# A first stage fed by 2 MB halves of the modulation weights and single K tiles, and precedence for emptying the mixers' PSUM banks

## The chip, the cores and the metric

One core of a Trainium2 chip runs the whole program. The metric is the device time of one execution in microseconds (us). TensorE (PE) multiplies, VectorE (DVE) and ScalarE (ACT) compute elementwise, GpSimd (POOL) does a little, and SyncE (SP) issues the DMAs. Every engine runs its own queue in order and waits at semaphores for the others.

## The reference

Two layers over 1024 tokens of width 2048, all in float32. In each layer:

```
mod = silu(c) @ w_mod + b_mod;  shift, scale, gate = split(mod, 3)
h   = rms_norm(x, g_pre) * (1 + scale) + shift
a_q, a_k, a_v, s_u, s_v, c_q, c_k, c_v, c_g, z = split(h @ w_in)
y_a = sliding_window_attention(rope(a_q), rope(a_k), a_v, sinks)     # 16 heads of 64, window 128
y_b = gelu(s_u) * (causal w_s @ layer_norm(gelu(s_v)) + b_s)          # chunks of 128
y_c = rms_norm(gated_linear_attention(c_q, c_k, c_v, log_sigmoid(c_g @ w_up + b) / 16), gla_norm_g)
out = (concat(y_a, y_b, y_c) * silu(z)) @ w_out
x   = x + gate * rms_norm(out, g_post)
```

## The kernel before

The work is cut into four phases: two layers, and in each two halves of 512 tokens. A phase has an input part (`in_phase`) and an output part (`out_phase`). Both are made of column groups: for each of 16 K tiles of 128 input features, four (or fewer) PSUM banks of the pool `pj` (6 banks) get three matmuls each. Three, because float32 is kept by splitting: each weight tile and each activation tile is cut into a high part (a cast on ACT, L368 for weights) and a low part (a subtraction on DVE, L369), and high x high, high x low and low x high are summed. `mm_f` (L382 to L384) writes features by tokens, `mm_t` (L390 to L392) tokens by features. A split activation tile is called a slot, in pool `act`; the raw weights sit in pool `wraw` (2 buffers), the split ones in `whl` (3 buffers), fetched two K tiles at a time.

The mixers (attention, spatial gating, gated linear attention) are generators on lanes. `tick()` is called after each three matmuls of a group, and a lane goes on when the number of ticks that its generator last yielded has passed. `LAG` holds such distances for attention: after the scores of two blocks ("s"), before the transposes ("e"), and after each of the two blocks of transposes ("t"). The mixers' matmuls write to the two banks of pool `mx`, and DVE or ACT must empty a bank before the next mixer matmul can have it: the scores are taken by L498/L500 (ACT) and L501 (DVE), the transposes of the probabilities M (L533) by the multiplication with the mask into PT (L535, DVE), the products PT x v (L546) by L549 (ACT), the scores of the linear attention by L617 (DVE), its output after the transposes L558 by ACT.

The order in each engine's queue is set by a scheduler: it takes instructions as written, by precedence and by its own picture of what is ready. Code in `urgent()` gets a precedence higher by `PRIO`, 300 instructions. The splits of weights already stand in it.

The modulation of later chunks (`mod_chunk`, L225 on DVE) also runs on a lane, fed by loads `wm` of 256 KB.

The first stage is written apart. Layer 0 needs `acol` and `bcol` (scale and shift by feature) before any slot can be made, and these need 8 chunks of 4 MB of `w_mod`. PE multiplies them with silu(c) spread over 32 columns (`scb`), two K tiles a load of 512 KB (L1107), the four 32-row strips of one bank taking K tiles in turn; `mod_columns` transposes the sums (L197) and makes two columns of acol and bcol. Meanwhile x, loaded with tokens on the partitions, is squared and summed on ACT (L1054), scaled on POOL (L283), transposed on PE (L1084), scaled and shifted on DVE (L1086) and split. `work()` puts the projection of the first five output blocks (512 columns of group "kcq" and 128 of `w_ck`) between the products, one block of three matmuls at a time. The sixth block (128 more columns of `w_ck`) follows in `in_phase` by `proj_f(P)`. Then comes the group `w_vcg` of 272 columns.

After the group "zc" (the z of the linear attention), `gla_c` loads gla_norm_g into a tile of pool `t2`, multiplies it into z (L820) and that into the output (L822), and transposes the result (`tok_to_y`, L558). In the same stretch the second attention of the phase is at work.

## Time and profile before

| | us |
|---|---|
| median of 3 runs | 3127.75 (3121.66 to 3129.04) |
| profiled execution, its own time | 3122.08 |
| its span | 3120.4 |
| PE busy | 3042.7 (98%) |
| DVE busy | 1837.3 (59%) |
| ACT busy | 1206.2 (39%) |
| mean granted PE clock | 0.991 |
| DMA moved | 469 MB, mean 150 GB/s |

How to read what follows. A row of the timeline gives the start, the duration, the engine, the line of the kernel, the operation, the tile written and read, the shape, the count of merged instructions (x4), and in brackets how long the engine sat idle before it and what ended that. Matmuls are pipelined: the durations of neighbours overlap, and the distance of two starts is what one costs. A row of the stages gives from:to, the length, then busy time and count for PE, weight loads (PEld), DVE, ACT and POOL, the granted PE clock (1.00 is full), the share of time that the DMA engines were busy, and GB/s. A row of waits reads: who <- for whom: us in total, times, longest.

### The profile page before, as it was taken

What the parts mean: (1) busy time and instruction counts of PE and PEld (TensorE: products, weight loads), DVE (VectorE), ACT (ScalarE), POOL (GpSimd) and SP (SyncE); (2) the same over time, 40 slices, a digit from 0 to 9 for tenths busy, and PEclk for the clock granted to TensorE, in tenths of its full rate; (3) what the DMA queues carried; (4) which work ended last, traced back from release to release, by engine and by line L of the source; (5) the groups of instructions that cost most, each with busy time, mean ns of one, the idle gap of its engine ahead of it and who ended that gap; (6) DMA issues with size and microseconds to landing.
All of it is one profiled execution on the core that took longest, in us unless ns stands there. A gap on an engine that the chain in (4) does not pass through costs nothing.

```text
span 3120.4 us, 44382 instructions
## 1 busy us (share of the span) xinstructions
PE 3042.7 (98%) x17346; PEld 2448.0 (78%) x17346; DVE 1837.3 (59%) x2957; ACT 1206.2 (39%) x2399; POOL 43.4 (1%) x84
## 2 busy tenths in 40 slices
PE   6999999999999999999999999999999999999998
PEld 2477778888878787888888878788888888788886
DVE  3358768565676877745355676644346486663425
ACT  3145437332344443423234554432223544442323
POOL 2000000000000000000000000000000000000000
PEclk8999999999999999999999999999999999999999
DMA  9754446566676435544446323334446332343535
GB/s 330 240 163 140 145 135 206 169 203 203 200 237 197 131 120 178 173 135 149 122 123 190 95 75 94 115 109 142 119 124 203 97 89 85 108 120 113 164 107 165
DMA packets 224195, 468.99 MB, mean 150 GB/s; under 512 B 21584, under 2 KB 77296, under 8 KB 223984
## 3 DMA queue, kind: packets, MB, share of 16 engines
q1 hardware_dynamic: 223984, 466.15, 48.7%
q8 instruction: 136, 2.23, 0.3%
q14 instruction: 75, 0.61, 0.1%
HBM read 429.37 MB, written 36.70 MB: 149 GB/s over the span
## 4 chain that ended last, share of the span: by engine, by line
PE 82%; DVE 8%; DMA 5%; ACT 2%; issue 2%; SPq 0%; DVEq 0%; ACTq 0%
PE pj L382 13%; PE pj L383 12%; PE pj L384 12%; PE pj L390 12%; PE pj L392 12%; PE pj L391 12%; DMA wm<-in_w_mod_dram 2%; PE mx L546 2%; PE mx L492 2%; PE pj L1107 1%; DVE whl L369 1%; DMA t<-in_gla_norm_g_dram 1%; DVE ma L225 1%; DMA t<-in_x_dram 1%; PE mx L533 1%
## 5 line engine op out<-in xcount | busy, mean ns | idle before, releaser
L369 DVE TENSOR_TENSOR whl<-wraw,whl 128x1024 fp32r<-128x1024 f32 (+3 forms) x512 | 590.6, 1154 | 730.6 <-ACT whl L368 728.0
L368 ACT CAST whl<-wraw 128x1024 fp32r<-128x1024 f32 (+3 forms) x512 | 509.1, 995 | 1097.0 <-PE pj L392 515.5
L390 PE MATMUL pj<-whl,act 128*128 128x512 f32 (+1 forms) x2048 | 785.5, 384 | 1.0 <-ACT whl L368 1.0
L392 PE MATMUL pj<-whl,act 128*128 128x512 f32 (+1 forms) x2048 | 777.8, 380 | 0.0
L391 PE MATMUL pj<-whl,act 128*128 128x512 f32 (+1 forms) x2048 | 775.3, 379 | 1.2 <-DVE whl L369 1.2
L382 PE MATMUL pj<-act,whl 128*128 128x512 f32 x1904 | 751.6, 397 | 3.6 <-ACT whl L368 2.0
L383 PE MATMUL pj<-act,whl 128*128 128x512 f32 x1904 | 745.3, 391 | 0.3 <-DVE act L279 0.3
L384 PE MATMUL pj<-act,whl 128*128 128x512 f32 x1904 | 744.5, 391 | 0.5 <-DVE whl L369 0.5
L392 PEld LDWEIGHTS pj<-whl,act 128*128 128x128 f32 x2048 | 385.4, 188 | 73.2 <-issue 1.2
L390 PEld LDWEIGHTS pj<-whl,act 128*128 128x128 f32 x2048 | 385.3, 188 | 72.7 <-issue 5.6
L391 PEld LDWEIGHTS pj<-whl,act 128*128 128x128 f32 x2048 | 385.5, 188 | 68.5 <-DVE whl L369 1.9
L382 PEld LDWEIGHTS pj<-act,whl 128*128 128x128 f32 x1904 | 357.5, 188 | 101.3 <-issue 20.3
L384 PEld LDWEIGHTS pj<-act,whl 128*128 128x128 f32 x1904 | 358.1, 188 | 83.7 <-issue 7.1
L383 PEld LDWEIGHTS pj<-act,whl 128*128 128x128 f32 x1904 | 358.2, 188 | 77.7 <-issue 6.2
L225 DVE SCALAR_TENSOR_TENSOR ma<-wm,sc,ma 128x512 f32<-128x512 f32 x240 | 179.7, 749 | 102.5 <-DMA wm<-in_w_mod_dram 100.1
L517 ACT ACTIVATE M<-M,at_nm 128x128 f32<-128x128 f32 x256 | 99.4, 390 | 46.7 <-DVE at_nm L509 42.2
L535 DVE TENSOR_TENSOR PT<-mx,amask 128x1024 f32<-128x1024 f32 x64 | 78.1, 1220 | 22.6 <-PE mx L533 22.6
L1107 PE MATMUL pj<-wm,scb 128*32 128x512 f32 x256 | 67.0, 665 | 24.2 <-DMA wm<-in_w_mod_dram 24.2
L501 DVE COPY_PREDICATED M<-pmask,mx 128x256 f32<-128x256 uint8 x128 | 51.6, 442 | 57.3 <-ACT M L500 48.5
L546 PE MATMUL mx<-PT,v 128*64 128x128 f32 x960 | 68.4, 288 | 13.9 <-DVE PT L535 13.9
L546 PEld LDWEIGHTS mx<-PT,v 128*64 128x64 f32 x960 | 57.5, 143 | 28.3 <-DVE PT L535 16.3
L500 ACT COPY M<-mx 128x256 f32<-128x256 f32 x96 | 32.1, 375 | 101.0 <-PE mx L492 100.7
(230 smaller groups left out, 2421.9 us busy)
## 6 DMA issues: line engine op xcount, KB each, us to landing
wraw<-in_w_in_dram SPq DMA_DIRECT2D x312, 512.0 KB, 3.6
wraw<-in_w_out_dram SPq DMA_DIRECT2D x136, 512.0 KB, 3.6
wm<-in_w_mod_dram SPq DMA_DIRECT2D x256, 256.0 KB, 3.3
wm<-in_w_mod_dram SPq DMA_DIRECT2D x64, 512.0 KB, 6.2
y<-at SPq DMA_DIRECT2D x64, 256.0 KB, 2.7
q<-y SPq DMA_DIRECT2D x64, 256.0 KB, 3.3
q<-x SPq DMA_DIRECT2D x36, 256.0 KB, 2.8
wraw<-in_w_vcg_dram SPq DMA_DIRECT2D x32, 272.0 KB, 2.8
```

The lines of the kernel that those rows point to most:

```text
L225: V.scalar_tensor_tensor(acc, ws[k], sc[:, k:k + 1], acc, ALU.mult, ALU.add)
L368: S.copy(hl[:, 0], raw)
L369: V.tensor_tensor(hl[:, 1], raw, hl[:, 0].bitcast(F32), ALU.subtract)
L382: PE.matmul(ps, lhsT=whi, rhs=slot[:, 0], start=(k == 0), stop=False)
L383: PE.matmul(ps, lhsT=whi, rhs=slot[:, 1], start=False, stop=False)
L384: PE.matmul(ps, lhsT=wlo, rhs=slot[:, 0], start=False, stop=(k == NK - 1))
L390: PE.matmul(ps, lhsT=slot[:, 0, c], rhs=whi, start=(k == 0), stop=False)
L391: PE.matmul(ps, lhsT=slot[:, 0, c], rhs=wlo, start=False, stop=False)
L392: PE.matmul(ps, lhsT=slot[:, 1, c], rhs=whi, start=False, stop=(k == NK - 1))
L517: S.activation(Mf[:, k], Mf[:, k], AF.Exp, bias=nm[:, k:k + 1], scale=0.125, accum_out=den[:, k:k + 1])
L546: PE.matmul(yp[64 * p:64 * p + 64, n * P:(n + 1) * P], lhsT=vv[:, g * 64:g * 64 + 64], rhs=pts[p][:, w, n], start=(w == 0), stop=(w == 1 o ...
L1107: PE.matmul(mps[r:r + 32, :], lhsT=scb[:, k], rhs=w[:, kk], start=(k < 4), stop=(k >= 12))
```

## The change

The first stage is rewritten, and instructions that empty the mixers' banks get precedence.

First stage:
- x comes with features on the partitions (`x_f` now holds both halves), eight loads of 512 KB ahead of everything else; it stays in eight tiles of pool `act`. No transposes of x.
- The sum of squares: ACT squares, DVE adds pairs, PE sums over the partitions by eight products with ones into one bank. The root is taken over 512 columns (`r0`).
- The modulation's weights come as 16 halves of 2 MB (3 buffers), eight products in a row for each, into a bank of `mx`.
- The weights of the projection come one K tile at a time (512 columns of "kcq" and all 256 of `w_ck`), queued behind the halves. `project(k)` does all six blocks of a K tile, so `in_phase` has nothing left to do for `w_ck` in the first phase.
- `fill` scales by acol and r0 (DVE), casts the high part with the shift added (ACT) and makes the low part (DVE). All of it is in `urgent()`.
- The tables of sines and cosines for the first half are made after the sixth chunk.

Mixers: `urgent()` around the emptying of the scores, of the transposes into PT, of PT x v, of the transposes to y, of the linear attention's scores and outputs, and of the spatial gating; "t" in LAG goes from (3, 5) to (3, 8); `gla_c` waits 5 more ticks before its transposes.

```diff
-LAG = {"s": (3, 4), "e": 14, "t": (3, 5)}
+LAG = {"s": (3, 4), "e": 14, "t": (3, 8)}
...
-    def rsqrt(out, src, n):
+    def rsqrt(out, src, n, pool=sm):
...
-            dst = out if it == 2 else sm.tile([P, n], F32, tag="rq_y", name="rq_y")
+            dst = out if it == 2 else yv
...
-                for p in range(2):
-                    sp = sps[p]
...
+                with urgent():
+                    for p in range(2):
+                        sp = sps[p]
...
-                V.tensor_tensor(pt, tp.rearrange("p (n q) -> p n q", n=NT).unsqueeze(1).broadcast_to([P, 2, NT, P]),
-                                amask.unsqueeze(2).broadcast_to([P, 2, NT, P]), ALU.mult)
+                with urgent():
+                    V.tensor_tensor(pt, tp.rearrange("p (n q) -> p n q", n=NT).unsqueeze(1).broadcast_to([P, 2, NT, P]),
+                                    amask.unsqueeze(2).broadcast_to([P, 2, NT, P]), ALU.mult)
...
-        ps = ps[4:] + proj_f(P, slots) if pre else proj_f(256, slots)
-        ck = evac(2, hold, ps)
+        ck = evac(2, hold, ps[4:] if pre else proj_f(256, slots))
...
                 V.tensor_tensor(of, of, zt[n], ALU.mult)
                 yield 2
+            yield 5
             yield from tok_to_y(h, [o.rearrange("p h d -> p (h d)") for o in outs], 12)
...
+        xq = [act_p.tile([P, 2, H], F32, tag="act", name="xq") for _ in range(8)]
+        for c in range(8):
+            load(xq[c], a["x_f"][0, 2 * c:2 * c + 2].rearrange("j p t -> p j t"))
...
+        def first_load(k):
+            if k < NK:
+                r = wraw_p.tile([P, 1, 768], F32, tag="wraw", name="wraw")
+                load(r[:, 0, 0:512], a["w_in"][0, 0, :, k])
+                load(r[:, 0, 512:], a["w_ck"][0, :, k])
+                raw_q.append(r)
...
+        def mod_load(c, part):
             if c < 8:
...
+                w = st.tile([P, 8, 512], F32, name="wm0", bufs=3)
+                load(w, a["w_mod"][0, c, :, 8 * part:8 * part + 8])
                 ws.append(w)
...
+        for c in range(8):
+            sq = st.tile([P, 2, H], F32, name="sq", bufs=2)
+            S.activation(sq, xq[c], AF.Square)
+            s2 = st.tile([P, H], F32, name="s2", bufs=2)
+            V.tensor_tensor(s2, sq[:, 0], sq[:, 1], ALU.add)
+            PE.matmul(sums, lhsT=ones, rhs=s2, start=(c == 0), stop=(c == 7))
+        r0 = st.tile([P, H], F32, name="r0")
+        V.tensor_scalar(r0, sums, 1.0 / D, EPS, ALU.mult, ALU.add)
+        rsqrt(r0, r0, H, st)
...
+        def mod_products(mps, part):
+
+            w = ws.popleft()
+            for kk in range(8):
+                k = 8 * part + kk
+                r = 32 * (k % 4)
+                PE.matmul(mps[r:r + 32, :], lhsT=scb[:, k], rhs=w[:, kk], start=(k < 4), stop=(k >= 12))
+
+        def fill(c, mps):
+            acc = st.tile([P, 512], F32, name="mod_acc", bufs=2)
+            S.copy(acc, mps)
             mod_columns(0, c, acc, 4)
...
+                V.scalar_tensor_tensor(xt, xq[c][:, j], acol[0][:, k:k + 1], r0, ALU.mult, ALU.mult)
+                s = act_p.tile([P, 2, 512], F32R, tag="act", name="act")
+                S.activation(s[:, 0], xt, AF.Identity, bias=b)
+                V.scalar_tensor_tensor(s[:, 1], xt, b, s[:, 0].bitcast(F32), ALU.add, ALU.subtract)
...
         for c in range(8):
+            if c:
+                mod_load(c, 1)
+                first_load(2 * c - 1)
+            mps = mxt()
+            mod_products(mps, 0)
+            if c:
+                project(2 * c - 2)
+                mod_load(c + 1, 0)
+                first_load(2 * c)
+            mod_products(mps, 1)
             with urgent():
+                fill(c, mps)
+            if c:
+                project(2 * c - 1)
+            if c == 5:
+                for _ in rope_tables(0):
                     pass
+        first_load(NK - 1)
+        project(NK - 2)
+        project(NK - 1)
```

The same `urgent()` stands around the emptying L549, L560, L617 and the others named above.

What this does to the queues is shown at three places. Lines are numbered by each kernel's own text; for the rows shown the changed kernel's numbers are lower by one (L369 is L368, L546 is L547), or higher by two to four behind the new `urgent()` lines (L558 is L560, L820 and L822 are L824 and L826).

SP's queue at the start of the program, before. `wm` are the modulation's weights, `x` the tokens, `raw_a` and `raw_b` the weights of the first projection.

```order
L58 DMA wm_190<-in_w_mod_dram 128x1024
L58 DMA x_0_169<-in_x_dram 128x4x512
L58 DMA x_1_170<-in_x_dram 128x4x512
L58 DMA x_2_171<-in_x_dram 128x4x512
L58 DMA x_3_172<-in_x_dram 128x4x512
L58 DMA t_196<-in_positions_dram 128x512
L58 DMA raw_a<-in_w_in_dram 128x1024
L58 DMA raw_b<-in_w_ck_dram 128x2x128
L58 DMA wm_293<-in_w_mod_dram 128x1024
```

The same queue now, `xq` being x with features on the partitions.

```order
L57 DMA xq<-in_x_f_dram 128x2x512 x8
L57 DMA wm_187<-in_w_mod_dram 128x4096
L57 DMA wm_189<-in_w_mod_dram 128x4096
L57 DMA wm_191<-in_w_mod_dram 128x4096
L57 DMA wraw<-in_w_in_dram 128x512
L57 DMA wraw<-in_w_ck_dram 128x256
L57 DMA wm_300<-in_w_mod_dram 128x4096
L57 DMA wraw<-in_w_in_dram 128x512
```

Eight loads of the modulation stood ahead of x before; now all of x goes first, and each half of the modulation is followed by one K tile of weights.

DVE's queue behind the z group of the third phase, before: the two PT multiplications of an attention step, the z and norm products L820 and L822, and a split of weights.

```order
L535 TENSOR_TENSOR PT<-mx,amask 128x1024
L820 SCALAR_TENSOR_TENSOR hold<-hold,t_16620 128x512
L535 TENSOR_TENSOR PT<-mx,amask 128x1024
L822 TENSOR_TENSOR hold<-hold 128x512
L820 SCALAR_TENSOR_TENSOR hold<-hold,t_16620 128x512
L369 TENSOR_TENSOR whl<-wraw,whl 128x1024
```

And now.

```order
L536 TENSOR_TENSOR PT<-mx,amask 128x1024
L824 SCALAR_TENSOR_TENSOR hold<-hold,t_16396 128x512
L536 TENSOR_TENSOR PT<-mx,amask 128x1024
L826 TENSOR_TENSOR hold<-hold 128x512
L824 SCALAR_TENSOR_TENSOR hold<-hold,t_16396 128x512
L368 TENSOR_TENSOR whl<-wraw,whl 128x1024
```

The order is the same here, as in the second and fourth phase; in the first phase both PT multiplications now stand ahead of the first L824.

PE's queue at the same place, before: products PT x v (L546), the projection of the next group (L390 to L392) and the transposes of the linear attention's output (L558).

```order
L391 MATMUL pj<-whl,act 128x512
L392 MATMUL pj<-whl,act 128x512
L546 MATMUL mx<-PT,v 64x128
L390 MATMUL pj<-whl,act 128x512
L391 MATMUL pj<-whl,act 128x512
L546 MATMUL mx<-PT,v 64x128 x13
L392 MATMUL pj<-whl,act 128x512
L558 MATMUL mx<-ident,hold 128x128
L390 MATMUL pj<-whl,act 128x512
```

And now.

```order
L390 MATMUL pj<-whl,act 128x512
L391 MATMUL pj<-whl,act 128x512
L547 MATMUL mx<-PT,v 64x128 x14
L560 MATMUL mx<-ident,hold 128x128 x4
L389 MATMUL pj<-whl,act 128x512
L390 MATMUL pj<-whl,act 128x512
```

Counted from the last matmul of the z group, 24 to 26 projection matmuls stood ahead of the bulk of PT x v, and now 42; the four transposes that were spread between projection matmuls stand in one block behind it. At the end of the first query group of the last three phases, 54 projection matmuls stood between the last scores of the fourth attention step and its transposes, and 40 do now; the two blocks of transposes there stand together.

More of the change, by code (lines that the diff above doesn't have):

```diff
@@ L548, in attention @@
             yt = att()
-            S.activation(yt, yp, AF.Copy, scale=0.5)
+            with urgent():
+                S.activation(yt, yp, AF.Copy, scale=0.5)
             load(y_d[h][i], yt)
@@ L559, in tok_to_y @@
             yt = att()
-            S.copy(yt, tp)
+            with urgent():
+                S.copy(yt, tp)
             load(y_d[h][base + c], yt)
@@ L615, in put @@
             pv = ps.rearrange("p (n t) -> p n t", t=P)
[L616 to L618 removed]
+            with urgent():
+                for e, c in parts:
+                    V.copy_predicated(sts[p][e, :, c],
+                                      gmask[e, m, c].unsqueeze(1).broadcast_to(list(sts[p][e, :, c].shape)), pv[e, :, c])
         rows = [slice(64 * p, 64 * p + 64) for p in range(2)]
@@ L721, in gla_blocks @@
             ob = hold((P, 4, P))
-            S.copy(ob, op)
+            with urgent():
+                S.copy(ob, op)
             outs.append(ob)
@@ L1007, in hybrid_kernel @@
     with tc.tile_pool(name="start", bufs=1) as st:
+        load(mb[0], a["b_mod_col"][0])
+        load(gpc[0], a["g_pre"][0])
+        xq = [act_p.tile([P, 2, H], F32, tag="act", name="xq") for _ in range(8)]
+        for c in range(8):
+            load(xq[c], a["x_f"][0, 2 * c:2 * c + 2].rearrange("j p t -> p j t"))
         scb = st.tile([P, NK, 32], F32, name="scb")
         V.tensor_copy(scb, sc.unsqueeze(2).broadcast_to([P, NK, 32]))
-        xg = [st.tile([P, 4, NT, P], F32, name=f"x0_{g}") for g in range(4)]
@@ L1028, in first_split @@
-        def first_split(c):
-            if c < 8:
-                for raw, hls, cols in ((raw_a, hl_a, 512), (raw_b, hl_b, P)):
-                    r = raw.popleft()
-                    if cols == P:
-                        hl = st.tile([P, 2, KC, P], F32R, name="hl_b", bufs=2)
-                    else:
-                        hl = whl_p.tile([P, 2, KC, 512], F32R, tag="whl", name="whl")
-                    S.copy(hl[:, 0], r)
-                    V.tensor_tensor(hl[:, 1], r, hl[:, 0].bitcast(F32), ALU.subtract)
-                    hls.append(hl)
@@ L1077, in tail @@
-        def tail(c, acc):
-            mod_columns(0, c, acc, 4)
-            yield
-            for j in (2 * c, 2 * c + 1):
-                pt = mxt()
-                for t in range(NT):
-                    PE.transpose(pt[:, t * P:(t + 1) * P], xg[j // 4][:, j % 4, t], ident)
-                v = t2()
-                V.tensor_scalar(v, pt, acol[0][:, j:j + 1], bcol[0][:, j:j + 1], ALU.mult, ALU.add)
-                slots.append(split(v))
-                yield
-        todo = work()
-        rest = iter(())
@@ L1123, in hybrid_kernel, with first_split @@
-        for _ in todo:
-            pass
+        ws, raw_q, hl_q = deque(), deque(), deque()
+        def first_load(k):
[4 more added lines that the diff above has]
+                raw_q.append(r)
+        def first_split():
+            r = raw_q.popleft()
+            hl = whl_p.tile([P, 2, 1, 768], F32R, tag="whl", name="whl")
+            S.copy(hl[:, 0], r)
+            V.tensor_tensor(hl[:, 1], r, hl[:, 0].bitcast(F32), ALU.subtract)
+            hl_q.append(hl)
```

124 lines of the change are left out of this document (33 added, 91 removed).

## The prediction

> **What bounds the kernel now.** I read the page's first lines, then busy time by stage, then who ended TensorE's waits, then the timeline at the two places that these point to.
>
> ```profile
> span 3120.4 us, 44382 instructions
> ...
> core 0: us, PE busy (x) PEld busy (x) DVE busy (x) ACT busy (x) POOL busy (x), PEclk, DMA share, GB/s
> 0.00:30.40 30.40, 9.88 (x36) 1.78 (x37) 3.90 (x15) 13.87 (x36) 1.64 (x8) 0.85 0.91 341
> 30.40:60.00 29.60, 24.75 (x92) 10.20 (x94) 19.93 (x38) 8.92 (x13) 18.87 (x16) 0.81 0.92 339
> 60.00:163.60 103.60, 98.21 (x432) 44.47 (x428) 28.67 (x60) 17.39 (x29) 0.18 (x1) 1.00 0.72 232
> 550.00:3120.00 2570.00, 2535.91 (x14241) 2086.59 (x14239) 1487.42 (x2310) 969.23 (x1806) 15.44 (x36) 0.99 0.47 141
> ```
>
> From 550 us on PE is busy all the time at full clock: only fewer matmuls or fewer waits can gain there. In the first 60 us the DMA engines are full (share 0.91, 0.92) and PE is not. From 60 to 163.6 us it is the reverse: PE full, DMA share 0.72. So the first stage is paid twice, first in transfers and then in matmuls.
>
> ```profile
> PE pj L1107 <- DMA wm<-in_w_mod_dram: 24.2, 6, 12.5
> PE mx L546 <- DVE PT L535: 13.9, 4, 4.4
> ...
> PE mx L492 <- DVE hold L617: 3.1, 4, 1.2
> PE mx L630 <- DVE hold L617: 2.8, 2, 2.1
> PE mx L709 <- DVE M L501: 2.4, 2, 2.1
> PE mx L652 <- DVE M L501: 2.3, 2, 1.7
> PE mx L533 <- DVE M L520: 2.1, 3, 1.0
> ...
> PE pj L391 <- DVE whl L369: 1.2, 3, 0.6
> ```
>
> PE's waits in total, times, longest. The first row is the first stage. The others are the mixers: 13.9 us for PT, four times (once a phase), and 3.1 + 2.8 + 2.4 + 2.3 = 10.6 us for PSUM banks that DVE had not emptied. Waits for split weights (the last row) are next to nothing.
>
> **The first stage, part by part.**
>
> ```profile
> 14.17 0.14 PEld L1107 LDWEIGHTS pj<-wm,scb 128*32 128x32 f32 x4 [1.14 <-DMA wm<-in_w_mod_dram]
> 15.46 0.14 PEld L1107 LDWEIGHTS pj<-wm,scb 128*32 128x32 f32 x4 [1.15 <-DMA wm<-in_w_mod_dram]
> ...
> 90.64 1.06 PE L1107 MATMUL pj<-wm,scb 128*32 128x512 f32 x8
> 92.44 0.66 PE L197 MATMUL mx<-ident,mod_acc 128*128 128x128 f32 x4 [0.73 <-ACT mod_acc L1117]
> 92.93 0.60 PE L1084 MATMUL mx<-ident,x 128*128 128x128 f32 x4
> 93.46 1.05 PE L1107 MATMUL pj<-wm,scb 128*32 128x512 f32 x4
> 94.45 0.66 PE L1084 MATMUL mx<-ident,x 128*128 128x128 f32 x4
> ...
> 170.73 0.39 PE L383 MATMUL pj<-act,whl 128*128 128x512 f32 x1
> ...
> 179.34 0.39 PE L382 MATMUL pj<-act,whl 128*128 128x512 f32 x1
> ...
> 183.56 0.77 PE L390 MATMUL pj<-whl,act 128*128 128x272 f32 x4 [1.00 <-ACT whl L368]
> ```
>
> Transfers: the eighth load of 512 KB is used at 15.46 us, 1.29 us after the seventh. That is 406 GB/s, 5.1 us for 2 MB.
>
> Products of the modulation: a product shows as two records, and a load of 512 KB, two K tiles, makes x4. These two products take 93.46 to 94.45, 0.99 us. Four (x8), which fell together once at 90.64, last 1.06 us, as long as two: the four 32-column strips of the array run beside each other. Before, nearly all products come in twos. Now eight stand in a row, so a half chunk costs 2 x 0.99 = 1.98 us in place of 4 x 0.99.
>
> Projection: 38 matmuls from 170.73 to 179.34, 0.2266 us each. The stage ends where the 272-column group starts, 183.56.
>
> Removed from PE: 64 transposes of x (64 x 0.13 = 8 us, by the 0.53 us from 92.93 to 93.46 for four), and half of the products' time (64 x 0.99 = 63 becomes 32 x 0.99 = 32). The sixth output block of the projection only moves from behind the stage into it: 48 matmuls either way. Added: eight products with ones for the sums of squares, in the first 17 us in which PE waits for transfers, at nothing; if PE were not idle there they would cost some 8 us. POOL's scaling of x goes; nobody waits for it later. The root's temporaries in place of three tiles and the pool for them cost nothing: DVE runs them in order anyhow.
>
> The new path to the first projection, each with its row:
>
> ```profile
> 16.56 0.59 ACT L1117 COPY mod_acc<-pj 128x512 f32<-128x512 f32 x1 [13.34 <-PE pj L1107]
> 18.43 0.16 DVE L205 SCALAR_TENSOR_TENSOR acol<-mod_t,gpc 128x2 f32<-128x2 f32 x1
> ...
> 35.04 1.22 DVE L1037 TENSOR_TENSOR whl<-raw_a,whl 128x1024 fp32r<-128x1024 f32 x1
> 44.51 0.62 ACT L278 CAST act<-t 128x512 fp32r<-128x512 f32 x1 [5.73 <-DVE t L1086]
> ...
> 1962.95 1.28 DVE L822 TENSOR_TENSOR hold<-hold 128x512 f32<-128x512 f32 x2
> ```
>
> Eight loads of x take the place of the eight modulation loads: last at 15.5. Halves at 20.6, 25.7, 30.9, first K tile (384 KB, 0.96 us) at 31.8. The second half's products, at the clock of a mostly idle PE (0.81 to 0.85 in the stage rows; I take half): 25.7 + 4.0 = 29.7. Copy to acol: 16.56 to 18.59, 2.0 us: 31.7. The root over 512 columns, some twelve DVE passes of up to 0.64 us, is 8 us that end near 26 and are hidden; without that cover they would start the projection later by as much. Two scalings and two low parts on DVE, 4 x 0.64, and the weights' low part, 768/1024 x 1.22 = 0.92: 35.2. ACT's two high parts (0.62 each) lie beside them. I take 35.5.
>
> From there PE is never free: 16 K tiles x 18 matmuls x 0.2266 = 65.3; 13 half chunks x 1.98 = 25.7; seven times four transposes, 0.49 (92.44 to 92.93) and a wait for the copy between 0 and 0.73, taken as 0.3: 5.5; the last slots 0.5. SP: the store of the second sine waits on SP for ACT, which stands behind the copy of the seventh chunk, and the last half chunk and the last four K tiles' loads are queued behind that store. Issued some 2 us after that copy, the last half lands 5.1 + 1 + about 2 us later, and PE has about 11 us of work before it needs it: between 0 and 3 us, I take 1. The sine and cosine tables move from the first 40 us behind the sixth chunk: some 16 DVE passes of up to 0.64 us, 10 us, beside some 5 us of DVE's other work in a pair of K tiles that takes PE 12.9 us. That may come out up to 2 us late; it is in the 0 to 3 of SP. Sum 98.0. So the stage ends at 35.5 + 98.0 + 1.0 (the wait at 183.56 again; it could be 0 to 5, since the small loads of masks and sinks lost the sixth block's 11 us as cover and stand on SP among the first loads of that group) = 134.5, 49 us earlier. Ends: start at 33.5 at full clock and 1.85 us a half chunk give 53; start at 40 and SP's 3 us give 42.
>
> Do transfers keep up? A pair of K tiles and two halves is 4.98 MB, 12.2 us at 406 GB/s; PE's work for it is 36 x 0.2266 + 3.96 + 0.79 = 12.9 us. Just.
>
> The Trainium skill (DMA: Bandwidth & Descriptors, section Specifications) puts what one core draws from HBM at about 358 GB/s. By that rule a pair takes 13.9 us, PE waits 1.0 us in each of six and a half, and the sum would be 3066; the trace does not agree, 406 GB/s stand in the rows above.
>
> **The mixers, part by part.**
>
> ```profile
> L546 PE MATMUL mx<-PT,v 128*64 128x128 f32 x960 | 68.4, 288 | 13.9 <-DVE PT L535 13.9
> ...
> 456.08 1.33 PE L546 MATMUL mx<-PT,v 128*64 128x128 f32 x10 [4.01 <-DVE PT L535]
> ...
> 1216.18 2.19 PE L546 MATMUL mx<-PT,v 128*64 128x128 f32 x18 [4.39 <-DVE PT L535]
> ...
> 1958.94 1.31 PE L546 MATMUL mx<-PT,v 128*64 128x128 f32 x20 [2.50 <-DVE PT L535]
> ...
> 2699.81 1.46 PE L546 MATMUL mx<-PT,v 128*64 128x128 f32 x20 [2.98 <-DVE PT L535]
> ...
> 1957.07 0.69 DVE L820 SCALAR_TENSOR_TENSOR hold<-hold,t 128x512 f32<-128x512 f32 x1 [3.98 <-DMA t<-in_gla_norm_g_dram]
> ...
> 454.90:461.70 6.80, 5.62 (x34) 4.82 (x35) 6.80 (x10) 0.60 (x1) 0.00 (x0) 0.50 0.41 132
> 1216.00:1219.40 3.40, 3.22 (x30) 3.22 (x32) 3.40 (x6) 0.00 (x0) 0.00 (x0) 0.51 0.01 4
> 1960.10:1963.60 3.50, 3.50 (x19) 2.70 (x15) 3.50 (x6) 0.60 (x1) 0.00 (x0) 0.51 0.37 51
> 2700.80:2704.20 3.40, 3.40 (x21) 2.69 (x18) 3.40 (x6) 0.60 (x1) 0.00 (x0) 0.50 0.29 58
> ```
>
> All four waits have one cause: in DVE's queue L820 stands between the two PT multiplications and waits for the load of gla_norm_g (3.98 us at 1957.07), PT behind it. Each is followed by a stretch at half clock (the last four rows, cut where the granted clock changes): 17.1 us, 15.7 of them past the wait's end, so 7.8 us more. Together 13.9 + 7.8 = 21.7 us.
>
> The change does not move L820 behind PT in three of four phases; it moves the matmuls with PT. 42 projection matmuls stand ahead of them since the z group's end where 24 to 26 stood: 16 x 0.2266 = 3.6 us later, enough for 2.50 and 2.98, nearly for the others. But now the transposes of the linear attention's output (L558 before, L560 now) stand as one block right behind, where projection matmuls stood between them, and they need the last L822, which ended at 1964.23, 7.2 us after the load. In that phase PE gets to them at 1956.44 + 3.6 + 2.1 (a block of L546: 68.4/32) = 1962.1 and waits 2.1. I take 2.5 in each phase, 10 in all (ends 0 and 13.9), and half clock after two of them, 3.4 us. Gain 21.7 - 13.4 = 8, less 1 for the two scheduled blocks of PT: 7.
>
> The Trainium skill (TensorE: Matmul & The Clock Gate, section HAM oscillation) lets the clock fall only after idle gaps over about 3.4 us; by that rule the new waits would cost no clock and the sum would be 3057. The trace does not agree: the wait of 2.50 us at 1958.94 has its stretch at 0.51.
>
> Banks: 10.6 us, of which precedence can take all or none; DVE's queue still has loads to wait for. I take two thirds with the clock behind the longer ones, 9 (ends 0 and 14).
>
> New: the last attention block of the first query group is drained early, so 40 in place of 54 matmuls stand between its last scores and its transposes in three phases. That is 3.2 us less cover; L533 waits at most 1.0 now. I take 2 us in all (ends 0 and 9).
>
> **The sum.** -49 - 7 - 9 + 2 = -63 against the profiled execution's own 3122.08 us: 3059. That execution lies 5.7 us under the median of 3127.75, so I say 3060.
>
> **Rivals.** (1) Transfers set the first stage's pace, or precedence does nothing. At the 339 GB/s of the second stage row a pair takes 14.7 us, 1.8 more than PE, times 6.5 is 12: 3072. With no gain at the mixers: 3074. For it: 341 and 339 with full engines. Against: in those stretches the queue also held small loads, stores and gaps; the eight loads in a row run at 406. The limit in the Trainium skill (DMA: Bandwidth & Descriptors, section Specifications) is a milder form of this rival. (2) The products do not run four abreast: 13 x 1.98 = 26 us back, 3086. Against it stands the one x8 row. (3) All the mixers' waits go, with their clock: 21.7 + 14 in place of 14, and the upper gain of the stage, 53: 3033. (4) Slower: emptying ahead of the weight splits in DVE's queue delays these, and PE stops at each block of weights. There are some 480 splits past the first stage; it decides from 63/480 = 0.13 us each, and at 0.2 us the time is 3155. Against: DVE is busy 1487 of 2570 us, and PE waits 1.2 us in all for L391's splits.
>
> **How the numbers follow.** Forecast 3047 to 3070: 0.58. Rival 1, 3070 to 3080: 0.22. Rival 3: 0.10. Rival 2: 0.05. Rival 4 or some mishap of its size: 0.03; within 0.3% (9 us, about what a measurement of this kernel can tell): 0.02. So faster 0.95, same 0.02, slower 0.03. The range 3036 to 3084 leaves out the ends of rivals 2 to 4.
>
> **What would show it.** The 272-column group starts near 134.5 (42 to 53 us earlier); products as x16 in about 2 us; PE above 95% from 36 us on with clock 1.00; no row L547 <- PT over 1 us, but a new L560 <- DVE hold of some 2.5 us each phase; waits for L617 and L501 gone or small. Wrong if PE waits for wm after 40 us, if x16 takes 4 us, or if splits show among PE's waits.

## The result and the profile after

The changed kernel takes 3079.54 us (median of 4 runs, 3074.17 to 3081.88), the kernel before beside it 3126.2: a ratio of 0.9847, 95% interval 0.9834 to 0.986. It is faster by 47 us. The forecast was 3060 by a sum of -63 us, so 16 us of that gain did not come. The profiled execution has a span of 3078.4 us against 3120.4. Cut at the start of the four 272-column groups (one for each layer and half), the spans are:

| us | first stage | phase 1 | phase 2 | phase 3 | phase 4 |
|---|---|---|---|---|---|
| before | 183.6 | 757.9 | 757.9 | 740.0 | 681.1 |
| after | 136.6 | 756.7 | 764.8 | 738.9 | 681.4 |
| forecast | -49 | -14 for the four together | | | |
| measured | -46.9 | +5.0 for the four together | | | |

These spans are of one profiled execution each, and that of before is 4 us under its median of 3126.2. By the medians the time fell by 46.7 us with a first stage shorter by 46.9, so the rest is the same within 0.3 us. The first stage did nearly what was forecast, and the mixers gained nothing where they were to gain 14. First the stages (from:to, length, busy time and count of PE, PEld, DVE, ACT, POOL, granted clock, DMA share, GB/s):

```profile
36.00:106.00 70.00, 69.52 (x391) 41.64 (x390) 33.60 (x66) 18.69 (x26) 0.00 (x0) 1.00 0.96 396
106.00:122.00 16.00, 13.01 (x60) 8.78 (x64) 6.36 (x13) 4.94 (x8) 0.00 (x0) 0.89 0.72 241
```

From 36 to 106 us PE and the DMA engines are full at the same time; before, one was full while the other was not. The one stretch in which neither is full is 106 to 122 us. The timeline of PE shows its two holes, and the steps that lead to it:

```profile
35.01 0.50 PE L381 MATMUL pj<-act,whl 128*128 128x512 f32 x1 [1.48 <-ACT whl L1035]
...
39.36 1.92 PE L1076 MATMUL mx<-wm,scb 128*32 128x512 f32 x16
...
52.20 1.92 PE L1076 MATMUL mx<-wm,scb 128*32 128x512 f32 x16
...
107.67 0.50 PE L381 MATMUL pj<-act,whl 128*128 128x512 f32 x1 [2.16 <-ACT whl L1035]
...
121.64 1.50 PE L1076 MATMUL mx<-wm,scb 128*32 128x512 f32 x12 [1.31 <-DMA wm<-in_w_mod_dram]
...
136.64 0.28 PE L389 MATMUL pj<-whl,act 128*128 128x272 f32 x1
```

A half chunk is one row of sixteen records in 1.92 us, and from 39.36 to 52.20, one pair of K tiles, it is 12.84 us. What made the holes at 107.67 and 121.64 stands in the queues of ACT and SP:

```profile
104.98 1.28 ACT L177 ACT_TABLE_LOAD   x1 [7.34 <-DVE t L173]
...
106.81 0.81 ACT L1035 CAST whl<-wraw 128x768 fp32r<-128x768 f32 x1
...
106.93 3.10 SPq L57 DMA_DIRECT2D cs<-t  x2
...
111.37 0.35 SPq L57 DMA_DIRECT2D wm<-in_w_mod_dram  x1
```

ACT stood 7.34 us in front of the cosine's table load for DVE's passes, with the next weight copy behind it; the stores of the tables then held SP for 3.10 us, with the last half chunk behind them.

PE's waits of the changed kernel (in total, times, longest):

```profile
PE mx L560 <- DVE hold L826: 9.4, 11, 1.5
...
PE mx L491 <- DVE hold L621: 7.5, 3, 6.2
...
PE mx L533 <- DVE M L520: 4.5, 3, 2.8
PE pj L383 <- DVE whl L368: 3.7, 3, 1.6
...
PE pj L381 <- ACT t L435: 3.5, 2, 2.9
...
PE mx L634 <- DVE hold L621: 1.5, 1, 1.5
PE mx L547 <- DVE PT L536: 1.5, 2, 1.3
```

The wait for PT fell from 13.9 to 1.5 us, and the transposes behind it (L560) wait 9.4 us in its place. The banks of the linear scores (L621) are late by 7.5 + 1.5 us, most of it in one wait. New are 3.5 us for ACT's copy L435 and 3.7 us for the low parts of the weights, which cost 0.5 on that line before. Two single waits carry most of what is new:

```profile
505.00 0.79 PE L381 MATMUL pj<-act,whl 128*128 128x512 f32 x1 [2.91 <-ACT t L435]
...
501.90 0.31 ACT L263 ACTIVATE junk<-wm 128x128 bf16<-128x128 f32 x1 [1.82 <-DMA wm<-in_x_dram]
...
991.41 0.55 PE L491 MATMUL mx<-kh,qs 128*128 128x256 f32 x1 [6.18 <-DVE hold L621]
...
977.73 1.54 DVE L621 COPY_PREDICATED hold<-gmask,mx 32x128 f32<-32x128 uint8 x6
...
989.45 2.03 DVE L621 COPY_PREDICATED hold<-gmask,mx 32x128 f32<-32x128 uint8 x8
...
504.10:510.90 6.80, 5.90 (x14) 4.47 (x15) 4.48 (x10) 6.50 (x15) 0.00 (x0) 0.50 0.64 189
988.70:995.50 6.80, 4.09 (x15) 3.73 (x16) 3.58 (x12) 1.00 (x3) 0.00 (x0) 0.50 0.51 155
```

At 505.00, ACT had stood 1.82 us for a tile of x, for the second half's statistics (L263), and the urgent copy L435 came behind the squares that followed. At 991.41 DVE was busy without a gap from 977.73 on: the rope of the queries, query splits, weight splits and modulation passes lay between the two copies L621. At each of the two the clock was halved for 6.8 us, from 0.9 and 2.7 us before PE went on (the last two rows).

### The profile page after: what moved, and what is told of

Read it like the earlier page. It is cut to its first block, busy times and chain, and to the rows that moved or that the text cites. A ratio compares the mean times of both kernels' runs of the same rounds, so it can differ in the third digit from the quotient of the medians.

```text
span 3078.4 us, 44118 instructions
## 1 busy us (share of the span) xinstructions
PE 3005.8 (98%) x17298; PEld 2445.1 (79%) x17298; DVE 1840.0 (60%) x2956; ACT 1198.9 (39%) x2367; POOL 24.9 (1%) x68
## 4 chain that ended last, share of the span: by engine, by line
PE 81%; DMA 7%; DVE 7%; ACT 3%; issue 2%; SPq 0%; DVEq 0%; ACTq 0%
PE pj L381 13%; PE pj L382 12%; PE pj L383 12%; PE pj L389 12%; PE pj L391 12%; PE pj L390 12%; DMA wm<-in_w_mod_dram 4%; PE mx L491 2%; PE mx L547 1%; DVE whl L368 1%; DMA t<-in_gla_norm_g_dram 1%; DVE ma L224 1%; DMA wm<-in_x_dram 1%; PE mx L1076 1%; PE mx L533 1%
## 5 line engine op out<-in xcount | busy, mean ns | idle before, releaser
L368 DVE TENSOR_TENSOR whl<-wraw,whl 128x1024 fp32r<-128x1024 f32 (+2 forms) x504 | 587.2, 1165 | 706.1 <-ACT whl L367 705.2
L367 ACT CAST whl<-wraw 128x1024 fp32r<-128x1024 f32 (+2 forms) x504 | 506.0, 1004 | 1128.1 <-PE pj L391 576.1
L390 PE MATMUL pj<-whl,act 128*128 128x512 f32 (+1 forms) x2048 | 776.8, 379 | 0.0
L381 PE MATMUL pj<-act,whl 128*128 128x512 f32 x1920 | 763.4, 398 | 9.3 <-ACT whl L1035 3.6
L383 PE MATMUL pj<-act,whl 128*128 128x512 f32 x1920 | 749.2, 391 | 3.7 <-DVE whl L368 3.7
L382 PE MATMUL pj<-act,whl 128*128 128x512 f32 x1920 | 751.5, 391 | 0.0
L381 PEld LDWEIGHTS pj<-act,whl 128*128 128x128 f32 x1920 | 361.5, 188 | 109.3 <-issue 23.0
L390 PEld LDWEIGHTS pj<-whl,act 128*128 128x128 f32 x2048 | 386.1, 189 | 67.4 <-issue 1.2
L383 PEld LDWEIGHTS pj<-act,whl 128*128 128x128 f32 x1920 | 361.9, 188 | 82.1 <-DVE whl L368 5.0
L382 PEld LDWEIGHTS pj<-act,whl 128*128 128x128 f32 x1920 | 362.1, 189 | 71.7 <-issue 1.1
L224 DVE SCALAR_TENSOR_TENSOR ma<-wm,sc,ma 128x512 f32<-128x512 f32 x240 | 179.5, 748 | 117.0 <-DMA wm<-in_w_mod_dram 115.3
L491 PE MATMUL mx<-kh,qs 128*128 128x256 f32 (+1 forms) x256 | 67.7, 297 | 7.7 <-DVE hold L621 7.5
L491 PE MATMUL mx<-kl,qs 128*128 128x256 f32 (+1 forms) x256 | 66.1, 286 | 0.0
L547 PEld LDWEIGHTS mx<-PT,v 128*64 128x64 f32 x960 | 53.1, 137 | 15.1 <-issue 7.1
```

What stands on the lines that cost most here:

```text
L224: V.scalar_tensor_tensor(acc, ws[k], sc[:, k:k + 1], acc, ALU.mult, ALU.add)
L367: S.copy(hl[:, 0], raw)
L368: V.tensor_tensor(hl[:, 1], raw, hl[:, 0].bitcast(F32), ALU.subtract)
L381: PE.matmul(ps, lhsT=whi, rhs=slot[:, 0], start=(k == 0), stop=False)
L382: PE.matmul(ps, lhsT=whi, rhs=slot[:, 1], start=False, stop=False)
L383: PE.matmul(ps, lhsT=wlo, rhs=slot[:, 0], start=False, stop=(k == NK - 1))
```

## The experiments

All kernels were compared with the kernel before on the same chip, whose medians there were 3125.3 to 3126.8 us. "272" is the start of the first 272-column group in the profiled execution, "rest" its span behind that, against the 2936.8 us of before. "Rest by medians" is the difference of the two medians less the shift of "272" against 183.6; its interval is 3 to 6 us to either side.

| kernel | median us | ratio, 95% interval | 272 at | rest | rest by medians |
|---|---|---|---|---|---|
| changed kernel | 3079.54 | 0.9847 (0.9834 to 0.986) | 136.6 | +5.0 | +0.3 |
| stage_only | 3085.11 | 0.9865 (0.9851 to 0.988) | 135.8 | +15.2 | +6.9 |
| mixers_only | 3129.45 | 1.0008 (0.9999 to 1.0017) | 183.5 | +3.4 | +3.5 |
| spacing_only | 3088.45 | 0.9868 (0.9851 to 0.9886) | 135.7 | +16.8 | +10.3 |
| precedence_only | 3074.48 | 0.9826 (0.981 to 0.9842) | 135.7 | -6.6 | -3.7 |
| lane44_stage | 3087.07 | 0.9874 (0.9859 to 0.9889) | 135.5 | +14.9 | +8.4 |
| lane44_after | 3082.57 | 0.9858 (0.9841 to 0.9874) | 135.8 | +7.7 | +3.6 |
| lane44_prec | 3071.77 | 0.9826 (0.9811 to 0.9841) | 136.7 | -3.0 | -8.1 |
| ticks16_stage | 3085.39 | 0.987 (0.9854 to 0.9887) | 137.4 | +10.9 | +6.3 |
| wm4_stage | 3068.27 | 0.9809 (0.9792 to 0.9825) | 136.1 | -5.3 | -10.1 |
| strips | 3132.39 | 1.003 (1.0016 to 1.0043) | 191.3 | +1.2 | -0.6 |
| prec_gn | 3065.16 | 0.9808 (0.9789 to 0.9826) | 137.6 | -15.2 | -15.6 |
| gn_rope | 3057.41 | 0.9787 (0.9773 to 0.9802) | 134.8 | -16.9 | -19.1 |

The profiled execution of precedence_only is its fastest, 6.4 us under its median, and that of stage_only its slowest, 4.5 us over it; where the two columns differ, the last one is the better number for the size. Phases below are of the profiled executions.

### The parts alone

stage_only has the new first stage and the mixers as before; mixers_only has the old first stage and every edit of the mixers.

```diff
 stage_only, against the changed kernel
-LAG = {"s": (3, 4), "e": 14, "t": (3, 8)}
+LAG = {"s": (3, 4), "e": 14, "t": (3, 5)}
...
-            with urgent():
-                S.copy(yt, tp)
+            S.copy(yt, tp)
...
 mixers_only, against the changed kernel
-        ck = evac(2, hold, ps[4:] if pre else proj_f(256, slots))
+        ps = ps[4:] + proj_f(P, slots) if pre else proj_f(256, slots)
+        ck = evac(2, hold, ps)
```

> The new first stage alone; mixers' precedence, their spacing and the five extra ticks are as before. Theory A (the mixers' edits gave back what they took): the 272-column group starts at 136.6 us as in the full change, and the rest of the program takes what it took before, 2937 us, within 2: profiled span 3073 to 3076, 3 to 5 us below the full change. Theory B (the new first stage itself disturbs the program behind it, and the mixers' edits gain some 14 us as predicted): the rest takes 2950 to 2956, span 3087 to 3093.

> The old first stage with all edits at the mixers. Theory A: the first stage ends at 183.6, the rest takes 2940 to 2944 in place of 2937; the time is that of before within 0.3%. Theory B: the rest takes about 2923, span 3106. In both a wait of the transposes L560 for the product with z of 2 to 3 us a phase is there.

The stage alone brings the start of the first 272-column group 47.8 us forward and the time 42 us down by its ratio (0.0135 x 3126). Its profiled execution shows 15.2 us lost behind the stage, as theory B has it, nearly all in phase 2 (773.4 us against 757.9); by the medians the loss is 6.9 us. So part of the stage's gain was lost in code that it does not touch. The mixers' edits on the old stage gain nothing, as theory A has it; on the new stage they gain 5.6 us by the medians, which the overlapping intervals do not show for certain.

The longest single wait of the changed kernel, 6.18 us for a bank of the linear scores, is there in stage_only too:

```profile
993.82 0.55 PE L491 MATMUL mx<-kh,qs 128*128 128x256 f32 x1 [6.15 <-DVE hold L616]
```

In the kernel before, the longest wait for these banks is 2.1 us. So this one came with the new stage and not with the edits of the mixers.

The mixers' edits were then parted, on the new stage: spacing_only has `LAG["t"] = (3, 8)` and the `yield 5` without the new `urgent()`; precedence_only has the `urgent()` and the old spacing:

```diff
 precedence_only, against the changed kernel
-LAG = {"s": (3, 4), "e": 14, "t": (3, 8)}
+LAG = {"s": (3, 4), "e": 14, "t": (3, 5)}
...
-            yield 5
             yield from tok_to_y(h, [o.rearrange("p h d -> p (h d)") for o in outs], 12)
```

> The full change without the precedence at the mixers: only three more ticks ahead of PT x v, five more ahead of the transposes. Theory A says that single long waits decide, as the one of 6.2 us for a bank at 991 us in the full change; without precedence that one may go and the small bank waits of before (10.6 us) come back: rest 2930 to 2942. The wait of PT x v stays near nothing if spacing alone removes it (my step), and is 10 us or more if precedence did.

> The full change with the old spacing: (3, 5) ticks and no five extra. If precedence removes the bank waits as I took it, waits for the copies L501 and the linear scores' emptying are under 4 us in all (10.6 before). If the load of gla_norm_g ahead of PT is the cause of the PT wait and spacing what removed it, that wait is back with 10 to 14 us in all, with stretches at half clock behind it: rest 2940 to 2950.

PE's wait for PT in stage_only, then in spacing_only, then in precedence_only, with what DVE does at the load of gla_norm_g in the third phase of the two last, and at the end the same place in the changed kernel:

```profile
PE mx L545 <- DVE PT L534: 16.9, 7, 3.7
```

```profile
PE mx L545 <- DVE PT L534: 14.6, 5, 4.2
...
1923.90 1.29 DVE L818 SCALAR_TENSOR_TENSOR hold<-hold,t 128x512 f32<-128x512 f32 x2 [4.00 <-DMA t<-in_gla_norm_g_dram]
...
1928.65 1.22 DVE L534 TENSOR_TENSOR PT<-mx,amask 128x1024 f32<-128x1024 f32 x1
```

```profile
PE mx L491 <- DVE hold L621: 8.0, 3, 6.2
PE mx L560 <- DVE hold L826: 7.5, 6, 2.6
PE mx L547 <- DVE PT L536: 5.7, 4, 3.1
...
1906.49 1.22 DVE L536 TENSOR_TENSOR PT<-mx,amask 128x1024 f32<-128x1024 f32 x1
1910.02 1.29 DVE L824 SCALAR_TENSOR_TENSOR hold<-hold,t 128x512 f32<-128x512 f32 x2 [2.31 <-DMA t<-in_gla_norm_g_dram]
```

```profile
1915.96 0.69 DVE L824 SCALAR_TENSOR_TENSOR hold<-hold,t 128x512 f32<-128x512 f32 x1 [4.29 <-DMA t<-in_gla_norm_g_dram]
1916.57 1.22 DVE L536 TENSOR_TENSOR PT<-mx,amask 128x1024 f32<-128x1024 f32 x1
```

Spacing alone leaves the wait (14.6 of 16.9 us) and the time (3088.45 against 3085.11): in the third phase the second PT multiplication comes six instructions later behind the product that waits for the load (1928.65), where in stage_only it came right behind that product. Its rest is over what theory A gave (2930 to 2942 us), and the wait is as large as was expected if precedence is what removes it. Precedence alone takes 10.6 us off the median, by another way than the spacing: in all four phases both PT multiplications come ahead of the product that waits for the load (1906.49 and 1910.02), and the four waits at this place are gone. The 5.7 us that are left stand at other attention steps, 4.6 of them near 459 and 1224 us. Both together, the change, put the second PT back behind that product in three phases (1916.57), but precedence keeps it right behind, and by the spacing PE comes later and waits only 1.5 us in all. They are slower than precedence alone: 5 us by these medians, whose intervals overlap, and 10.8 us for the pair lane44_after and lane44_prec below, whose intervals only touch. So the spacing brings nothing alone, and beside precedence it seems to cost.

What was expected of precedence_only failed in both parts. The wait for PT was not back at 10 to 14 us, and the waits for banks of the attention's and the linear scores are not under 4 us: they sum to 11.6, against 11.4 in stage_only. On the new stage precedence took nothing from them.

### Is it the place of the modulation's lane?

The old first stage counted 16 ticks for the lanes with its last 128-column group; the new one has none. If the lane of the later modulation chunks had only slipped by that, one number would mend it:

```diff
-    start("mod", iter((60,)))
+    start("mod", iter((44,)))
```

It was set in stage_only, in the changed kernel and in precedence_only.

> New first stage, mixers as before (the kernel that ran at 3085, with phases of 758.3, 773.4, 739.9 and 680.4 us from one 272-column group to the next), and the lane of the modulation chunks starts 44 ticks in, in place of 60. The old first stage's last 128-column group counted 16 ticks for this lane and the new one has none, so with 60 the lane stands 16 ticks later against the phases; with 44 it stands where it stood before the change. Theory A (that shift is why everything behind the new first stage is some 15 us slower): the second phase comes back to 758 to 761, the wait of some 6 us for the linear scores near 990 is gone, time 3070 to 3075. Theory B (the shift is harmless, something else that the first stage leaves costs the time): phases within 3 us of 758, 773, 740 and 680, time 3083 to 3089.

> The changed kernel whole, with the lane of the modulation chunks 44 ticks in, in place of 60. Changed kernel: 3079.5, phases 756.7, 764.8, 738.9, 681.4. Theory A (the lane's shift of 16 ticks costs the time): second phase 758 or less, the waits near 505 and 991 gone, time 3066 to 3072. Theory B (not the lane): 3077 to 3082. A third reading, C: any shift of the lane only exchanges collisions for others; then the phases change by some us each in both directions and the time stays within 5 us of 3079.

> Changed kernel with the old spacing (precedence alone, 3074.5 with 60 ticks, phases 751.3, 765.6, 736.4, 676.9), lane 44 ticks in. Theory A: second phase 752 to 757, no wait of 6 us near 985, time 3060 to 3066. Theory B: 3072 to 3077. Theory C (other collisions in exchange): phases change in both directions, 3070 to 3079.

No. All three times miss theory A. The loss of stage_only moved from phase 2 (773.4 to 762.4) to phase 1 (758.3 to 768.9) and stayed as large; lane44_after and lane44_prec are some 3 us from their pairs. Theory C's picture, collisions in exchange, fits all three best, but no run separates it from other causes.

ticks16_stage goes further and counts the 16 ticks for all lanes, which puts every lane where it stood before:

```diff
+        if pre:
+            for _ in range(16):
+                tick()
         ck = evac(2, hold, ps[4:] if pre else proj_f(256, slots))
```

> New first stage, mixers as before (3085.1 with phases of 758.3, 773.4, 739.9 and 680.4; before 757.9, 757.9, 740.0 and 681.1), and 16 ticks of the lanes' clock counted ahead of the first 272-column group, where the old first stage counted them with its last 128-column group: every lane, the key rope's too, stands against the projections as before the change. Theory A2 (all lanes together shifted by 16 ticks cost the 15 us; the modulation lane alone had moved them only from the second phase to the first): both first phases within 3 us of 758, time 3069 to 3075. Theory B (the position of the lanes is not it; what the shorter first stage leaves behind costs the time, so that the instruction streams collide in another way at whatever offset): the first two phases together stay 10 to 20 us longer than before, time 3081 to 3089.

No again: phases 769.9 and 758.7, 3085.39 us. That speaks against the lanes' offset as the cause, and it made the traces easy to compare, since the lanes now stood the same. DVE in this kernel, then in the kernel before, at the same place behind the first 272-column group (started at 137.4 and 183.6):

```profile
164.23 1.54 DVE L224 SCALAR_TENSOR_TENSOR ma<-wm,sc,ma 128x512 f32<-128x512 f32 x2 [1.81 <-DMA wm<-in_w_mod_dram]
168.45 0.75 DVE L224 SCALAR_TENSOR_TENSOR ma<-wm,sc,ma 128x512 f32<-128x512 f32 x1 [1.55 <-DMA wm<-in_w_mod_dram]
...
175.58 0.75 DVE L224 SCALAR_TENSOR_TENSOR ma<-wm,sc,ma 128x512 f32<-128x512 f32 x1 [2.30 <-DMA wm<-in_w_mod_dram]
...
183.50 1.37 DVE L584 TENSOR_TENSOR_SCAN hold<-ones,t 128x128 f32<-128x128 f32 x4
```

```profile
209.91 0.75 DVE L225 SCALAR_TENSOR_TENSOR ma<-wm,sc,ma 128x512 f32<-128x512 f32 x1 [0.68 <-DMA wm<-in_w_mod_dram]
...
212.91 0.75 DVE L225 SCALAR_TENSOR_TENSOR ma<-wm,sc,ma 128x512 f32<-128x512 f32 x1 [1.11 <-DMA wm<-in_w_mod_dram]
...
224.40 1.37 DVE L585 TENSOR_TENSOR_SCAN hold<-ones,t 128x128 f32<-128x128 f32 x4
```

L224 (L225) adds one K tile of a later modulation chunk, and DVE, which takes its queue in order, stops there for the tile's transfer: 1.55, 1.81 and 2.30 us where it was 0.68 and 1.11. The linear attention's gates (L575) and their scan come behind. The scan starts 46.1 us into the phase (183.50 - 137.4) in place of 40.8 (224.40 - 183.6), and with it the scores and their banks.

wm4_stage tests that: ticks16_stage with four buffers for these tiles, loaded three ahead.

```diff
-        fetch(0)
+        for k in range(3):
+            fetch(k)
         for k in range(NK):
-            if k + 1 < NK:
-                fetch(k + 1)
+            if k + 3 < NK:
+                fetch(k + 3)
...
-    for name, bufs in (... ("wm", 2), ...
+    for name, bufs in (... ("wm", 4), ...
```

> New first stage, old mixers, lanes' clock as before (3085.4, phases of 769.9, 758.7, 738.2 and 680.9; before 757.9, 757.9, 740.0 and 681.1), and the later modulation chunks load their K tiles into four buffers, three ahead, in place of two buffers and one ahead. In the kernel without this edit, 26 to 38 us behind the start of the first 272-column group, DVE waits 1.5 to 2.3 us for each of several K tiles of modulation, where it waited 0.5 to 1.1 us before the change, and the gates of the linear attention stand behind them in its queue; their scan ends up 5.2 us later against the projections. Theory C (these late transfers are what the new first stage costs its successor): DVE waits for the modulation tiles under 0.5 us there, the first phase comes back to 756 to 762, time 3070 to 3078. Theory B (the late transfers are harmless; the order in DVE's queue and its coincidences decide): first phase still 766 or more, or the loss comes up in another phase, time 3080 to 3090.

Phases 757.5 and 754.6, 3068.27 us, 17 us less, and 2 us under theory C's range. PE's idle time in the first phase went from 24.4 to 14.6 us; before the change it was 13.8. DVE's waits for these tiles in the whole kernel: before the change, in ticks16_stage, and then in wm4_stage, and there the scan, 39.8 us into the phase (175.90 - 136.1):

```profile
DVE ma L225 <- DMA wm<-in_w_mod_dram: 100.1, 81, 5.5
```

```profile
DVE ma L224 <- DMA wm<-in_w_mod_dram: 112.8, 87, 4.9
```

```profile
DVE ma L225 <- DMA wm<-in_w_mod_dram: 27.6, 32, 2.0
...
175.90 1.37 DVE L585 TENSOR_TENSOR_SCAN hold<-ones,t 128x128 f32<-128x128 f32 x4
```

So DVE's standing for these transfers costs time behind the new stage, and with the tiles early the loss of the first phase is gone. But the buffers give more than was lost: by the medians the rest goes from 6.3 us longer than before to 10.1 us shorter, so more than half of the gain is no loss of the new stage. The kernel before had 100.1 us of the same waits, and in the first 116 us behind the 272-column group 10.7 us against 12.7 in ticks16_stage (2.9 in wm4_stage). Whether it too would gain by the buffers was not run. That these waits are the whole of the new stage's loss is therefore not shown, and why they come at other moments behind the new stage stays open.

### Do four column strips run side by side?

strips gives each strip four neighbouring K tiles, so that products in a row fall into the same strip:

```diff
-                r = 32 * (k % 4)
-                PE.matmul(mps[r:r + 32, :], lhsT=scb[:, k], rhs=w[:, kk], start=(k < 4), stop=(k >= 12))
+                r = 32 * (k // 4)
+                PE.matmul(mps[r:r + 32, :], lhsT=scb[:, k], rhs=w[:, kk], start=(k % 4 == 0), stop=(k % 4 == 3))
```

> The changed kernel, with the modulation products of four neighbouring K tiles in the same column strip of TensorE (strip k // 4) in place of four strips in turn (k % 4); the sums over the four strips are the same. Theory 1 (four strips run side by side, and that is why 8 products take some 2 us): 8 products in one or two strips take 3.5 to 4 us, the first stage gets 13 x 1.6 to 2 = 21 to 26 us longer less what waits it covers, 272-column group at 152 to 163, time 3095 to 3106. Theory 2 (strips do not matter, the products are short of themselves): 2 us for 8, time 3076 to 3083.

The same sixteen records take 5.37 us in place of 1.92:

```profile
41.93 5.37 PE L1076 MATMUL mx<-wm,scb 128*32 128x512 f32 x16
```

The 272-column group starts 54.7 us later. Thirteen of the sixteen half chunks stand behind the start of the projection: 13 x 3.45 = 44.9 us. The projection itself starts 2.6 us later, and the transposes now wait 4.2 us for the copy of the sums, for which they did not wait in the changed kernel.

So strips in turn carry more than the whole gain of the first stage: without them it ends at 191.3 us, later than before. The expectation was right in kind and too low in size: it took the pairs of before (0.99 us for two products) for products in a row, but at 5.37 us for eight in a row two would take 1.34, so those pairs already overlapped.

### Taking the remaining waits away

prec_gn is precedence_only with gla_norm_g loaded once per layer behind the first stage:

```diff
         def gla_c():
-            gn = t2()
-            load(gn.rearrange("p (h d) -> p h d", h=4), a["gla_norm_g"][l:l + 1].unsqueeze(1).broadcast_to([P, 4, P]))
+            gn = gnorm[l]
```

> Precedence alone (3074.5; it still shows 5.7 us of waits for PT and 7.5 us for the gated output before the transposes of the linear attention), with gla_norm_g loaded once per layer right behind the first stage into buffers of its own, in place of a load in each phase for which DVE waits some 4 us. Theory 1 (that load is what both waits hang on): PT under 1.5 and the gated output under 2, time 3058 to 3068. Theory 2 (the scores and the weight splits in DVE's queue set both waits, the load only shows up there): both waits within 2 us of what they were, time 3072 to 3077.

```profile
PE mx L492 <- DVE hold L622: 7.8, 3, 6.2
...
PE mx L548 <- DVE PT L537: 4.8, 3, 2.5
```

9.3 us faster than precedence_only by the medians, though the intervals of the ratios (0.9789 to 0.9826 and 0.981 to 0.9842) overlap. The wait for the gated output is gone from the list (7.5 us in precedence_only); that for PT hardly changed (5.7 to 4.8). Each theory has one of the two waits right: the load set the gated output's, not the rest of PT's, which in precedence_only stood at other places already. The wait of 6.2 us for a bank of the linear scores is still there.

gn_rope adds the tables of sine and cosine in steps from the third chunk on, in place of one block behind the sixth:

```diff
-            if c == 5:
-                for _ in rope_tables(0):
-                    pass
+            if c >= 2:
+                next(tables, None)
```

(and once more between the two projections of a chunk, with buffers of its own).

> Precedence alone with gla_norm_g loaded once per layer (3065.2), and the first half's sine and cosine tables taken apart into steps that are spread from the third chunk on, in buffers of their own, in place of one block behind the sixth chunk. Theory 1 (the waits of 2.2 us near 107 for ACT's weight copies behind the sine, of 1.2 us near 121 for the last half chunk, and the half clock behind the first come from that block): 272-column group at 131 to 133 in place of 135.7 to 137.6, time 3058 to 3063. Theory 2 (transfers are late there anyway, and the sine waits elsewhere as long): 272-column group within 1 us of 136, time 3063 to 3068.

```profile
134.79 0.39 PE L389 MATMUL pj<-whl,act 128*128 128x272 f32 x1 [2.67 <-ACT t L769]
...
133.61 0.64 ACT L367 CAST whl<-wraw 128x544 fp32r<-128x544 f32 x1 [8.40 <-DMA wraw<-in_w_vcg_dram]
134.16 1.07 ACT L769 COPY t<-pj 128x512 f32<-128x512 f32 x2
```

3057.41 us, the fastest that was run, and faster than the kernel before and the changed one (0.9787 against 0.9847, intervals apart); against prec_gn it is 7.7 us by the medians, with overlapping intervals. The hole near 107 is gone, but the group starts at 134.8, not at 131 to 133: PE now waits 2.67 us there, since ACT stood 8.40 us for the group's own weights with the emptying of the projection's banks behind. Theory 1 has the hole right, theory 2 that a late transfer stands there anyway; neither has the start of the group. Four buffers for the modulation tiles together with this were not run.

## Why the prediction was right and wrong

**First stage, -49 forecast, -46.9 measured.** The start of the projection (35.5 against 35.01), the half chunk (1.98 against 1.92), the pair (12.9 against 12.84) and four strips abreast came out. Mis-sized is the term for SP and the tables, "between 0 and 3 us, I take 1": it measured 2.16 at 107.67, 1.31 at 121.64, and the clock of 0.89 in the 16 us from 106 on costs another 1.8: 5.3 us together, beyond its range. Its cause was named for SP; that ACT's weight copies would stand behind the sine was not. The 1.0 us for the wait at the 272-column group did not come.

**Transfers (rival 1).** The DMA engines moved 396 GB/s for 70 us beside a full PE, and a pair took 12.84 us. At the Trainium skill's about 358 GB/s (DMA: Bandwidth & Descriptors, section Specifications) it would have taken 13.9 us, an estimate; the trace does not agree. It agrees with the section Bandwidth of that page in the Trainium skill, which gives 425 GB/s to one core alone and about 358 to each of two.

**Place behind the z group, -7.** In size it holds: the waits went from 13.9 to 1.5 + 9.4 (10 was taken for the new one), and of the stretches at half clock behind them two of 3.4 us are left, as forecast (1924.0 is shown below). In the changed kernel its mechanism is there too: in three phases PT stands behind the load as before, and PE comes later. What the prediction left out is precedence: without it the spacing pushes PT further back and 14.6 us of waits stay, and alone it puts PT ahead of the load in all four phases. So the spacing is not what the gain needs, and together the two only trade PT for L560.

**Banks, -9.** This is the step that failed. The four rows summed to 10.6 us before; now there are 7.5 + 1.5 for the linear scores and 1.0 for the attention's, with 6.8 us of half clock at the longest. "I take two thirds" stood on no row. On the old stage the edits do take some of it (6.5 us are left in mixers_only), on the new one precedence takes nothing (11.6 against 11.4). At 991.41 some 10 us of other DVE work still stood between two copies, the same instructions in the same order as in stage_only, which has no precedence.

**L533, +2.** 2.1 went to 4.5.

**What was not in the sum.** ACT's copy L435 (3.5 us, and 6.8 us at half clock) is in spacing_only too (1.9 us), but not in stage_only or precedence_only, so it goes with the spacing. The weights' low parts (0.5 to 3.7 us) are as late in stage_only (3.8 us), so this is not rival 4, which blamed the emptying ahead of them; precedence_only has 1.6. Larger is what the new stage does to the code behind it with the old mixers, +6.9 us by the medians (+15.2 in the profiled execution): the prediction costed the rest of the program as if it only began earlier.

**The total.** The sum of -63 gives 3059 for an execution that lies 5.7 us under the median, so by its own working the forecast of the median is 3065; 3060 is a slip. Without any gain at the mixers that becomes 3079, and 3079.54 was measured: the second half of rival 1, though not for its reason, since precedence did move DVE. That the time lies inside the stated range is the first stage's doing. Two of the signs of being wrong showed, both small: PE waited 1.31 us for `wm` after 40 us, and splits stand among its waits.

## What to carry to other kernels

Where an engine takes its queue in order, a side stream that waits for its transfers delays everything behind it: here two more buffers, filled three tiles ahead, took 85 us of such waits from DVE and 17 us from the time. Price a precedence from the rows of the queue that stand ahead of the instruction, not as a share of the wait. Try the parts of a change one at a time: here the spacing gains nothing alone and seems a loss beside precedence, and the three together show neither. And set a profiled execution beside its median before taking a difference of two profiles for a cost.

## What the runs showed that was not expected

Sixteen records of 32-column products take 1.92 us over four strips in turn and 5.37 us in one strip after another, a factor of 2.8 from the index alone. And the clock falls behind waits that are short each: after 0.93, 1.48 and 0.27 us within 4 us PE has half the clock for 3.4 us, in the changed kernel at

```profile
1920.77 0.33 PE L560 MATMUL mx<-ident,hold 128*128 128x128 f32 x1 [0.93 <-DVE hold L826]
1922.58 0.33 PE L560 MATMUL mx<-ident,hold 128*128 128x128 f32 x1 [1.48 <-DVE hold L826]
1923.18 0.33 PE L560 MATMUL mx<-ident,hold 128*128 128x128 f32 x1 [0.27 <-DVE hold L826]
...
1924.00:1927.40 3.40, 3.40 (x13) 3.03 (x13) 0.73 (x1) 1.55 (x4) 0.00 (x0) 0.50 0.27 93
```

No gap over 1.5 us is near. The Trainium skill (TensorE: Matmul & The Clock Gate, section HAM oscillation) asks for idle gaps over about 3.4 us; this trace does not agree. It agrees with the next section of that page in the Trainium skill (A second HAM failure mode: psum-queue depth-cycling), which tells of another kernel where frequent short idles make the clock swing.
